# A Strassen mixer on one core: the second half's norm moved ahead of two early weight pairs, right factors made in the order of their products, four early pairs

## The chip, the cores and the metric

The kernel runs on one core of a Trainium2 chip. The core has a matrix engine (PE, with its weight loads PEld), a vector engine (DVE), an activation engine (ACT), a general engine (POOL) and a queue that issues DMAs (SP). Each engine takes its instructions strictly in the order of its own list, and waits for semaphores of the others. The metric is the time of one execution on the device in microseconds. Time before: 1500.17 us, the median of 3 runs (1498.93 to 1500.93).

## What is computed

A two-layer encoder trunk on 1024 tokens of width 1024, all in fp32. Layer 0 is attention and retention, layer 1 a gated short convolution; after each comes a cross-attention into 256 memory tokens. The change touches the entry of layer 1:

```
def conv_mixer(xn, w_in, conv_w, conv_b, w_out):
    gb, gc, u, gate = jnp.split(xn @ w_in, 4, axis=-1)      # w_in: 1024 x 4096
    z = gc * u
    conv = conv_b + (three taps over z along the tokens)
    y = gb * conv * jax.nn.silu(gate)
    return y @ w_out

x = x + conv_mixer(rmsnorm(x, o_norm), o_w_in, ...)          # x: sum of layer 0 and its cross-attention
```

## The kernel before

Activations lie transposed, 128 of the width on the partitions and the tokens along the free axis. An fp32 product is three passes on PE (`mm3`, L185 to L191): each operand is split in a high part, a cast by ACT, and a low part, a subtraction on DVE (`split`, L204 to L206), and hi*hi, hi*lo and lo*hi are summed. One such matmul is 128x128 by 128x512.

The product `xn @ w_in` is made in 16 **weight pairs** of two 128-column weight tiles each, and each pair as a 2x2 block product after Strassen and Winograd with 7 products instead of 8 (`strassen`, L611). The left factors come from the weights: A11, A12, A22 and the sums S1 to S4 (L99 to L102, on POOL), each cast by ACT and split by DVE (L106, L107) into a page; three `whi` and three `wlo` pages hold six factors in advance. The right factors come from the activations, the same ones for all 16 pairs: B11 and B21 from the first 512 tokens, and T1, T2, T3, B22, T4 from both halves (`right_factors`, L564; T1 = B12 - B11, T2 = B22 - T1, T3 = B22 - B12, T4 = B21 - T2). One product is 4 blocks of 3 matmuls, so 12 matmuls; a whole pair is 84.

The layer's input comes out of the previous output projection in two halves of 512 tokens (`out_proj_halves`, L301), each followed by its norm (`norm_half`, L265: add the last squares, split the sum, two matmuls by ones at L256 and L257, then Ln, Exp and Square on ACT and three steps on DVE, which give R) and by `right_factors` of that half, which first multiplies the tiles by gain and R (L575). With the first half done, only the products A11*B11 and A12*B21 of a pair can be made. Three pairs are begun with these two (`conv_start`, `EARLY` = 3): 24 matmuls each, from a weight tile that is loaded whole for this purpose. Everything that is left of these pairs ("late" products: T1, T2, T3, B22, T4 with their weight sums) and of the other 13 follows in `conv_in`.

Raw weight tiles go through two buffers (`wraw`), so the next pair's tiles are loaded once the present pair's sums and A22 are done with them. A product that adds to a sum in PSUM on which a copy (`kept`, by ACT, L623) has to be taken first waits for that copy.

The order on every engine is set by a scheduler at build time that simulates a timeline; the code's order is its starting point, and `issue_after` (used by the change) tells it what must be issued first. It decides where pieces of neighbouring pairs are interleaved.

Of the kernel before, what the change touches and what calls it, by code (L numbers as in the profile page):

```python
# [31 lines left out]
EARLY = 3  # L32
# [8 lines left out]
class Weights:  # L41
# [5 lines left out]
    FACTORS = ("A11", "A12", "S2", "S1", "S3", "S4", "A22")  # L47
# [88 lines left out]
class Trunk:  # L136
# [48 lines left out]
    def mm3(self, o, ah, al, bh, bl, first, last, more=False):  # L185
# [5 lines left out]
        mm(o, al, bh, start=False, stop=last, skip_group_check=more)  # L191
# [12 lines left out]
    def split(self, hi, lo, src, eng=None):  # L204
        self.nc.scalar.copy(hi, src)  # L205
        (eng or self.nc.vector).tensor_tensor(lo, src, hi.bitcast(F32), op=ALU.subtract)  # L206
# [15 lines left out]
    def rsqrt(self, var, out=None):  # L222
# [10 lines left out]
        nc.vector.tensor_tensor(out, t, r, op=ALU.mult)  # L233
# [17 lines left out]
    def mean(self, ones, sq):  # L251
# [5 lines left out]
        self.nc.tensor.matmul(ps, ones, w[:, 1, :n], start=False, stop=True)  # L257
# [306 lines left out]
    def right_factors(self, x, gain, h, out):  # L564
# [7 lines left out]
        for f in ("B11", "B21") if h == 0 else ("B12", "B22"):  # L572
# [5 lines left out]
        def split(f, src):  # L578
            for k in range(4):
# [8 lines left out]
                self.split(hi, lo, src[k])  # L588
                out.setdefault(f, []).append((hi, lo))

        if h == 0:
            split("B11", B["B11"])
            split("B21", B["B21"])
            return
# [15 lines left out]

    def strassen(self, B, out, early=False):  # L611
# [3 lines left out]
        def product(ps, f, first, weights=None):  # L615
            ah, al = weights or self.w.take()
            for k, (bh, bl) in enumerate(B[f]):
                c = slice(k * P, k * P + P)
                self.mm3(ps, ah[:, c], al[:, c], bh, bl, first and k == 0, k == 3, not first)
# [54 lines left out]
    def conv_start(self, B):  # L674

        self.started = []
        for i in range(EARLY):
            d = self.buf("v", "z" if i % 2 else "y1")
            self.started.append((d, self.times(B, d, None if i % 2 else AF.Silu, i)))
            next(self.started[-1][1])  # L680

    def conv_in(self, B):
# [3 lines left out]
        def pair(i):  # L686
# [5 lines left out]
            for _ in steps:  # L692
                pass
# [356 lines left out]
```

## Time and profile before

| | |
|---|---|
| median of 3 runs | 1500.17 us |
| the profiled execution | 1498.43 us |
| its span, first to last instruction | 1496.5 us |
| PE busy | 1442.0 us, 96% |
| DVE / ACT / POOL busy | 59% / 42% / 23% |
| PE busy from 820 to 860 us | 16.93 us of 40 |

The span is split by engine and in stretches of time; the granted clock of PE stands beside each stretch (1.00 is 2.4 GHz, 0.50 is 1.2 GHz). PE's matmuls are recorded with 0.39 us each, but at full speed the next one starts 0.227 us after the one before, so starts are what is to be counted.

### The profile page before, as it was taken

The page shows a single profiled execution, that of the slowest core. Times are in us where ns is not written, and L with a number is a line of the kernel's source. Part 1 is how long each engine was busy: PE and PEld are TensorE (multiplying, and loading weights), DVE is VectorE, ACT ScalarE, POOL GpSimd, SP SyncE. Part 2 cuts the span into 40 slices and gives each one's busy share as a digit, 9 for nine tenths or more (in the row PEclk, how much of TensorE's full clock was granted, in tenths as well). Part 3 has the DMA queues.
Part 4 walks back from the last instruction along what each step waited for, and adds up shares of the span by engine and source line. Part 5 has one row for each costly group of instructions (what it writes and reads, how often), then busy time and mean ns, then how long its engine had stood idle before and what let it go on. Part 6 is the DMA issues. An engine that isn't in the chain of part 4 may idle for free.

```text
span 1496.5 us, 18719 instructions
## 1 busy us (share of the span) xinstructions
PE 1442.0 (96%) x7218; PEld 1219.2 (81%) x7218; DVE 880.5 (59%) x1286; ACT 633.2 (42%) x1140; POOL 337.3 (23%) x205
## 2 busy tenths in 40 slices
PE   8999999999989999999999499999999999999996
PEld 6888888888788888888887288888888888888996
DVE  7656765566673356446465756666666336446555
ACT  6435662333363244345344333333344325335554
POOL 2300103233301210000114544444440120000233
PEclk9999999999999999999999599999999999999999
DMA  5411104211464521104754021111126532111464
GB/s 214 160 51 29 56 29 141 81 61 43 141 214 152 166 78 42 40 29 142 237 179 147 28 68 50 54 55 57 57 71 227 196 127 71 29 41 39 127 206 152
DMA packets 51482, 152.86 MB, mean 102 GB/s; under 512 B 6337, under 2 KB 14657, under 8 KB 50881
## 3 DMA queue, kind: packets, MB, share of 16 engines
q1 hardware_dynamic: 51392, 151.66, 31.8%
q8 instruction: 57, 0.93, 0.3%
q14 instruction: 33, 0.26, 0.1%
HBM read 122.28 MB, written 25.17 MB: 99 GB/s over the span
## 4 chain that ended last, share of the span: by engine, by line
PE 79%; DMA 6%; DVE 6%; POOL 3%; issue 3%; ACT 2%; SPq 0%; DVEq 0%; POOLq 0%; ACTq 0%
PE psd L189 16%; PE psd L191 16%; PE psd L190 16%; PE pssc L191 6%; PE pssc L190 6%; PE pssc L189 6%; PE psa L190 4%; PE psa L189 4%; PE psa L191 4%; DMA wraw<-w_o 1%; DMA swap<-bk 1%; PE pssc L367 1%; DMA swap<-bq 1%; PE psa L397 1%; PE psa L843 1%
## 5 line engine op out<-in xcount | busy, mean ns | idle before, releaser
L189 PE MATMUL psd<-xh,whi 128*128 128x512 f32 (+2 forms) x1096 | 414.1, 381 | 7.7 <-ACT whi L87 7.2
L190 PE MATMUL psd<-xl,whi 128*128 128x512 f32 (+2 forms) x1096 | 414.5, 379 | 0.0
L191 PE MATMUL psd<-xh,wlo 128*128 128x512 f32 (+2 forms) x1096 | 414.0, 379 | 0.0
L189 PEld LDWEIGHTS psd<-xh,whi 128*128 128x128 f32 x1096 | 206.5, 188 | 43.2 <-ACT whi L87 7.7
L191 PEld LDWEIGHTS psd<-xh,wlo 128*128 128x128 f32 x1096 | 206.2, 188 | 34.8
L190 PEld LDWEIGHTS psd<-xl,whi 128*128 128x128 f32 x1096 | 206.6, 189 | 34.0
L87 ACT CAST whi<-wraw 128x1024 fp32r<-128x1024 f32 (+1 forms) x134 | 139.8, 1044 | 212.3 <-PE psd L190 133.7
L249 POOL TENSOR_TENSOR ssq<-ssq,xold 128x512 f32<-128x512 f32 (+2 forms) x54 | 84.0, 1556 | 576.8 <-ACT xold L247 503.0
L88 DVE TENSOR_TENSOR wlo<-wraw,whi 128x1024 fp32r<-128x1024 f32 (+1 forms) x134 | 167.9, 1255 | 77.2 <-ACT whi L87 75.7
L106 ACT CAST wf<-ws 128x512 fp32r<-128x512 f32 x64 | 39.6, 622 | 138.5 <-PE pssc L191 81.5
L189 PE MATMUL pssc<-T,wf 128*128 128x512 f32 x180 | 71.7, 398 | 19.6 <-ACT T L205 9.9
L291 DVE TENSOR_TENSOR xnew<-psd,xold 128x512 f32<-128x512 f32 x32 | 21.9, 690 | 96.0 <-PE psd L191 92.6
L190 PE MATMUL pssc<-T,wf 128*128 128x512 f32 x180 | 71.8, 399 | 1.4 <-DVE T L206 1.4
L191 PE MATMUL pssc<-T,wf 128*128 128x512 f32 x180 | 71.0, 395 | 0.0
L247 ACT ACTIVATE xold<-xnew 128x512 f32<-128x512 f32 (+2 forms) x63 | 36.4, 580 | 70.2 <-DVE xnew L291 35.1
L107 DVE TENSOR_TENSOR wf<-ws,wf 128x512 fp32r<-128x512 f32 x64 | 49.6, 777 | 27.2 <-ACT wf L106 27.2
L107 DVE TENSOR_TENSOR wf<-wraw,wf 128x512 fp32r<-128x512 f32 x42 | 59.5, 1418 | 5.2 <-ACT wf L106 5.2
L189 PEld LDWEIGHTS pssc<-T,wf 128*128 128x128 f32 x180 | 34.4, 191 | 28.5 <-ACT T L205 10.3
L205 ACT CAST Th<-psa 128x512 fp32r<-128x512 f32 (+1 forms) x62 | 34.3, 588 | 54.5 <-PE psa L843 29.8
L99 POOL TENSOR_TENSOR ws<-wraw 128x512 f32<-128x512 f32 x16 | 38.9, 2429 | 69.2 <-DMA wraw<-w_o_in 61.9
L206 DVE TENSOR_TENSOR Tl<-psa,Th 128x512 fp32r<-128x512 f32 (+1 forms) x62 | 41.7, 687 | 21.4 <-ACT Th L205 21.1
L278 DVE TENSOR_TENSOR q<-psd,R 128x512 f32<-128x512 f32 x32 | 22.1, 690 | 53.9 <-PE psd L191 53.8
(319 smaller groups left out, 2975.4 us busy)
## 6 DMA issues: line engine op xcount, KB each, us to landing
wraw<-w_o SPq DMA_DIRECT2D x40, 512.0 KB, 3.9
wraw<-w_o_in SPq DMA_DIRECT2D x35, 512.0 KB, 3.6
wraw<-w_e_in SPq DMA_DIRECT2D x25, 512.0 KB, 3.9
wraw<-w_k SPq DMA_DIRECT2D x16, 512.0 KB, 4.1
xold<-x SPq DMA_DIRECT2D x16, 512.0 KB, 5.2
wraw<-w_v SPq DMA_DIRECT2D x16, 512.0 KB, 3.7
x<-xnew SPq DMA_DIRECT2D x16, 512.0 KB, 2.6
wraw<-w_q SPq DMA_DIRECT2D x16, 512.0 KB, 3.5
```

The lines of the kernel that those rows point to most:

```text
L87: self.nc.scalar.copy(hi[:, c], raw[:, c])
L88: self.nc.vector.tensor_tensor(lo[:, c], raw[:, c], hi[:, c].bitcast(F32), op=ALU.subtract)
L99: tt(F["S1"], F["A21"], F["A22"], op=ALU.add)
L106: self.nc.scalar.copy(hi, src)
L107: self.nc.vector.tensor_tensor(lo, src, hi.bitcast(F32), op=ALU.subtract)
L189: mm(o, ah, bh, start=first, stop=False, skip_group_check=more)
L190: mm(o, ah, bl, start=False, stop=False, skip_group_check=more)
L191: mm(o, al, bh, start=False, stop=last, skip_group_check=more)
L205: self.nc.scalar.copy(hi, src)
L206: (eng or self.nc.vector).tensor_tensor(lo, src, hi.bitcast(F32), op=ALU.subtract)
L247: nc.scalar.activation(sq, x, AF.Square)
L249: eng.tensor_tensor(self.ssq[:, a:b], self.ssq[:, a:b], sq, op=ALU.add)
```

## The change

`EARLY` goes from 3 to 4: a fourth pair is begun before the second half's right factors are there, with one more weight tile loaded whole. The early pairs 2 to 4 are to be issued behind the first early pair and behind the second half's norm (its ones-matmuls, its last activation and its last DVE step). `right_factors` of the second half makes each factor whole in turn: T1 (scale B12, subtract, split), T2 (scale B22, subtract, split), T3, B22, T4, each behind the one before. The products follow that order, T1's ahead of T2's in all pairs, and so the weight sum S1 comes ahead of S2. The sums of the first pair of `conv_in` are made by DVE instead of POOL. Unchanged lines are cut:

```diff
-EARLY = 3
+EARLY = 4
-    FACTORS = ("A11", "A12", "S2", "S1", "S3", "S4", "A22")
+    FACTORS = ("A11", "A12", "S1", "S2", "S3", "S4", "A22")
-            tt = self.nc.gpsimd.tensor_tensor
+            tt = (self.nc.vector if self.order[i][3:] else self.nc.gpsimd).tensor_tensor
...
-        for f in ("B11", "B21") if h == 0 else ("B12", "B22"):
+        def normed(f):
             for k in range(4):
...
-        for k in range(4):
-            tt(T1[k], B["B12"][k], B["B11"][k], op=sub)
-            tt(T2[k], B["B22"][k], T1[k], op=sub)
-        split("T2", T2)
-        split("T1", T1)
-        for k in range(4):
-            tt(T3[k], B["B22"][k], B["B12"][k], op=sub)
-        split("T3", T3)
-        split("B22", B["B22"])
-        for k in range(4):
-            tt(T4[k], B["B21"][k], T2[k], op=sub)
-        split("T4", T4)
+        def t1():
+            normed("B12")
+            for k in range(4):
+                tt(T1[k], B["B12"][k], B["B11"][k], op=sub)
+            return split("T1", T1)
+        def t2():
+            normed("B22")
+            for k in range(4):
+                tt(T2[k], B["B22"][k], T1[k], op=sub)
+            return split("T2", T2)
...
+        with ExitStack() as behind:
+            for make in (t1, t2, t3, lambda: split("B22", B["B22"]), t4):
+                last = make()
+                behind.enter_context(self.tc.issue_after(last.ins))
+                behind.enter_context(self.tc.issue_after(self.last_cast.ins))
...
-        product(a, "T2", False)
-        u2 = kept(a)
         c = self.ps("a")
         product(c, "T1", True)
         p5 = kept(c)
+        product(a, "T2", False)
+        u2 = kept(a)
         product(a, "T3", False)
...
+        with ExitStack() as behind:
+            for i in range(EARLY):
...
+                if i == 0:
+                    for x in (self.last_mean, self.last_act, self.last_rsqrt):
+                        behind.enter_context(self.tc.issue_after(x.ins))
+        self.last_early = self.last_mm
...
-                for i in range(0, len(o_in), 2)]
+                + ((True,) if i == 0 else ()) for i in range(0, len(o_in), 2)]
```

What this makes of the order shows at three places. In the rows a tile's last number is its own; `psa`, `psd` and `pssc` are PSUM tiles, `wf` a left factor, `ws` a tile of two sums, `xnew` the activations that are scaled in place.

**PE, around the norm's two ones-matmuls (L256, L257).** Before, they stand in the second early pair (`pssc_876`):

```order
L190 MATMUL pssc_876_6975<-B11_846_6611,whi83_6886 128x512
L256 MATMUL psa_868_6922<-sq2_867_6921,mean_dr_77 128x512
L191 MATMUL pssc_876_6975<-B11_846_6611,wlo83_6887 128x512
L189 MATMUL psd_877_6976<-B21_847_6614,whi83_6886 128x512
L190 MATMUL psd_877_6976<-B21_847_6614,whi83_6886 128x512
L257 MATMUL psa_868_6922<-sq2_867_6921,mean_dr_77 128x512
```

Now, right behind the last matmul of the first early pair (`psd_873`):

```order
L191 MATMUL psd_873_6937<-B21_850_6623,wlo82_6850 128x512
L256 MATMUL psa_868_6922<-sq2_867_6921,mean_dr_77 128x512
L257 MATMUL psa_868_6922<-sq2_867_6921,mean_dr_77 128x512
L189 MATMUL pssc_876_6973<-B11_843_6598,whi83_6886 128x512
L190 MATMUL pssc_876_6973<-B11_843_6598,whi83_6886 128x512
```

They stand 11 and 14 rows further ahead; three early pairs stand behind them now.

**DVE, from the scaling of the second half on, and POOL's sums.** Before, all eight tiles are scaled (L575), then the differences of all factors follow, and the first split (L206) comes 16 rows behind the last scaling:

```order
L575 SCALAR_TENSOR_TENSOR xnew_797_5992<-xnew_797_5992,gains_70,R_1_83 128x512
L575 SCALAR_TENSOR_TENSOR xnew_798_5993<-xnew_798_5993,gains_70,R_1_83 128x512
L599 TENSOR_TENSOR xnew_791_5986<-xnew_791_5986 128x512
L660 TENSOR_TENSOR y1_881_7016<-psd_883_7018,kept_884_7037 128x512
...
L608 TENSOR_TENSOR xnew_795_5990<-xnew_795_5990,T2_885_7061 128x512
L206 TENSOR_TENSOR T2_887_7071<-T2_885_7061,T2_887_7071 128x512
```

Now four tiles are scaled, and T1's first split comes eight rows later, with two of the sums of the first pair's weights (L99, L101) among them:

```order
L575 SCALAR_TENSOR_TENSOR xnew_794_5989<-xnew_794_5989,gains_70,R_1_83 128x512
L679 TENSOR_TENSOR z_875_6972<-psd_877_6974,kept_878_6995 128x512
L604 TENSOR_TENSOR xnew_791_5986<-xnew_791_5986 128x512
L604 TENSOR_TENSOR xnew_792_5987<-xnew_792_5987 128x512
L604 TENSOR_TENSOR xnew_793_5988<-xnew_793_5988 128x512
L99 TENSOR_TENSOR ws_882_7013<-wraw86_1_6981 128x512
L101 TENSOR_TENSOR ws_882_7013<-wraw86_0_6979,wraw86_1_6981 128x512
L604 TENSOR_TENSOR xnew_794_5989<-xnew_794_5989 128x512
L206 TENSOR_TENSOR T1_891_7099<-xnew_791_5986,T1_891_7099 128x512
```

On POOL the four sums of the first pair are gone, and the second pair's (`ws_908`, `ws_909`, from `wraw87`) stand first.

**PE, where the second pair's late products begin, and ACT's copy ahead of T3.** Before, two matmuls of the second pair (`pssc_876`, left factor `wf90`) stand in the middle of the first pair's T1 (`psa_906`):

```order
L189 MATMUL psa_906_7165<-T1_890_7086,wf86_6986 128x512
L189 MATMUL pssc_876_6975<-T2_887_7071,wf90_7148 128x512
L190 MATMUL pssc_876_6975<-T2_887_7071,wf90_7148 128x512
L190 MATMUL psa_906_7165<-T1_890_7086,wf86_6986 128x512
L191 MATMUL psa_906_7165<-T1_890_7086,wf86_6986 128x512
```

Now two of the second pair's T1 (`psa_913`, left factor `wf91`, its S1) stand between the first pair's B22 and its T4:

```order
L191 MATMUL psa_907_7171<-B22_902_7152,wf89_7059 128x512
L189 MATMUL psa_913_7274<-T1_891_7099,wf91_7185 128x512
L190 MATMUL psa_913_7274<-T1_891_7099,wf91_7185 128x512
L189 MATMUL pssc_872_6936<-T4_903_7159,wf90_7172 128x512
L190 MATMUL pssc_872_6936<-T4_903_7159,wf90_7172 128x512
```

On ACT the copy for which the first pair's T3 waits stands behind all casts of T3 and B22 now:

```order
L205 CAST T3_898_7140<-xnew_794_5989 128x512
L205 CAST B22_899_7143<-xnew_795_5990 128x512
L205 CAST B22_900_7146<-xnew_796_5991 128x512
L205 CAST B22_901_7149<-xnew_797_5992 128x512
L205 CAST B22_902_7152<-xnew_798_5993 128x512
L642 COPY kept_911_7217<-pssc_872_6936 128x512
L205 CAST T4_903_7159<-xnew_795_5990 128x512
```

So 17 late matmuls of the first pair stood ahead of the second pair's first two before, and 48 stand there now. In the last eleven pairs (the sixth to the sixteenth) the order is now: nine matmuls of T1, T4 of the pair before (12), three of T1, T2 (12), two of the next pair's first product, B22 (12, with S4), eight of the next pair's first product, T3 (12). Before, B22 and its S4 came 49 matmuls behind the T4 of the pair before.

## Rows read from the trace of the kernel before

**Rows 1.** Two stretches: busy PE, PEld, DVE, ACT, POOL, then PE's clock, DMA, GB/s.

```profile
820.00:860.00 40.00, 16.93 (x42) 10.54 (x41) 32.22 (x52) 16.60 (x30) 21.50 (x4) 0.62 0.09 26
860.00:1496.50 636.50, 624.20 (x3048) 534.72 (x3046) 367.82 (x447) 256.67 (x431) 173.03 (x111) 0.99 0.30 96
```

**Rows 2.** PE's waits, whole span: for whom, us in total, times, longest.

```profile
PE pssc L189 <- ACT T L205: 9.9, 1, 9.9
PE pssc L189 <- ACT wf L106: 9.0, 1, 9.0
```

**Rows 3.** PE in order of time: start, us, operation, and idle time before it.

```profile
804.45 0.39 PE L189 MATMUL pssc<-B,whi 128*128 128x512 f32 x1
...
818.05 0.39 PE L190 MATMUL psd<-B,whi 128*128 128x512 f32 x1
...
821.40 0.39 PE L191 MATMUL psd<-B,wlo 128*128 128x512 f32 x1
...
841.50 0.63 PE L190 MATMUL psa<-T,wf 128*128 128x512 f32 x1
...
843.63 0.63 PE L189 MATMUL psa<-T,wf 128*128 128x512 f32 x1
...
853.28 0.80 PE L189 MATMUL pssc<-T,wf 128*128 128x512 f32 x1 [9.03 <-ACT wf L106]
...
858.16 0.50 PE L189 MATMUL pssc<-T,wf 128*128 128x512 f32 x1 [0.68 <-ACT kept L623]
```

**Rows 4.** Single microseconds; behind the five engines' times stands PE's granted clock.

```profile
824.00:825.00 1.00, 0.00 (x0) 0.00 (x0) 1.00 (x3) 0.00 (x0) 0.00 (x0) 0.54 0.00 0
...
858.00:859.00 1.00, 0.83 (x4) 0.70 (x5) 0.35 (x2) 1.00 (x3) 0.00 (x0) 0.90 0.00 0
```

**Rows 5.** DVE in order of time, from the last early weight tile on.

```profile
805.55 1.23 DVE L88 TENSOR_TENSOR wlo<-wraw,whi 128x1024 fp32r<-128x1024 f32 x1 [0.21 <-ACT whi L87]
...
808.07 0.69 DVE L206 TENSOR_TENSOR sq<-ssq,sq 128x512 fp32r<-128x512 f32 x1 [0.69 <-ACT sq L205]
...
817.42 0.69 DVE L231 SCALAR_TENSOR_TENSOR rt<-psa,rt 128x512 f32<-128x512 f32 x1 [0.68 <-ACT rt L230]
...
821.37 5.39 DVE L575 SCALAR_TENSOR_TENSOR xnew<-xnew,gains,R 128x512 f32<-128x512 f32 x8
826.67 0.69 DVE L599 TENSOR_TENSOR xnew<-xnew 128x512 f32<-128x512 f32 x1
...
841.11 2.49 DVE L206 TENSOR_TENSOR T<-xnew,T 128x512 fp32r<-128x512 f32 x4
...
847.13 1.89 DVE L206 TENSOR_TENSOR T<-xnew,T 128x512 fp32r<-128x512 f32 x3
```

**Rows 6.** ACT in order of time, at the norm and at the splits.

```profile
814.85 0.62 ACT L106 CAST wf<-ws 128x512 fp32r<-128x512 f32 x1 [2.33 <-POOL ws L100]
815.38 0.69 ACT L228 ACTIVATE rs<-psa,eps 128x512 f32<-128x512 f32 x1
...
837.57 2.17 ACT L205 CAST B<-xnew 128x512 fp32r<-128x512 f32 x4
...
857.53 0.58 ACT L623 COPY kept<-pssc 128x512 f32<-128x512 f32 x1 [0.24 <-PE pssc L191]
```

**Rows 7.** POOL in order of time: the sums of the first and the second pair.

```profile
810.58 1.29 POOL L99 TENSOR_TENSOR ws<-wraw 128x512 f32<-128x512 f32 x1 [8.04 <-DMA wraw<-w_o_in]
...
832.35 17.79 POOL L99 TENSOR_TENSOR ws<-wraw 128x512 f32<-128x512 f32 x1 [16.16 <-DMA wraw<-w_o_in]
850.10 1.26 POOL L101 TENSOR_TENSOR ws<-wraw,wraw 128x512 f32<-128x512 f32 x1
```

**Rows 8.** Raw weight tiles, 780 to 900 us: times from a DMA's issue to its landing.

```profile
DMA to landing us min/median/max: 3.4/3.6/7.2
```

**Rows 9.** Sum tiles: cast and low part of a left factor, ns min/median/max over 64 of each.

```profile
L106 ACT CAST wf<-ws x64: 617/622/631, 811.9 to 1127.4; 128x512 fp32r<-128x512 f32 x64
L107 DVE TENSOR_TENSOR wf<-ws,wf x64: 673/692/1384, 812.6 to 1128.1; 128x512 fp32r<-128x512 f32 x64
```

More of the change, by code (lines that the diff above doesn't have):

```diff
@@ L190, in mm3 @@
         mm(o, ah, bl, start=False, stop=False, skip_group_check=more)
-        mm(o, al, bh, start=False, stop=last, skip_group_check=more)
+        self.last_mm = mm(o, al, bh, start=False, stop=last, skip_group_check=more)
     def dense(self, xs, done, parts=((0, H), (H, S)), tags="d"):
@@ L204, in split @@
     def split(self, hi, lo, src, eng=None):
-        self.nc.scalar.copy(hi, src)
-        (eng or self.nc.vector).tensor_tensor(lo, src, hi.bitcast(F32), op=ALU.subtract)
+        self.last_cast = self.nc.scalar.copy(hi, src)
+        return (eng or self.nc.vector).tensor_tensor(lo, src, hi.bitcast(F32), op=ALU.subtract)
     def split_k(self, src, gain=None, two=False):
@@ L232, in rsqrt @@
         nc.vector.tensor_scalar(t, t, -0.5, 1.5, ALU.mult, ALU.add)
-        nc.vector.tensor_tensor(out, t, r, op=ALU.mult)
+        self.last_rsqrt = nc.vector.tensor_tensor(out, t, r, op=ALU.mult)
         return out
@@ L256, in mean @@
         self.nc.tensor.matmul(ps, ones, w[:, 0, :n], start=True, stop=False)
-        self.nc.tensor.matmul(ps, ones, w[:, 1, :n], start=False, stop=True)
+        self.last_mean = self.nc.tensor.matmul(ps, ones, w[:, 1, :n], start=False, stop=True)
         return ps
@@ L587, in split @@
                     hi, lo = t[:, :H], t[:, H:]
-                self.split(hi, lo, src[k])
+                last = self.split(hi, lo, src[k])
                 out.setdefault(f, []).append((hi, lo))
+            return last
         if h == 0:
-            split("B11", B["B11"])
-            split("B21", B["B21"])
+            for f in ("B11", "B21"):
+                normed(f)
+                split(f, B[f])
             return
@@ L597, in right_factors, with t3, t4 @@
         T2 = [t[:, i, :] for t in (self.buf("T", "T2", (P, 2, H)) for _ in range(2)) for i in range(2)]
-        for k in range(4):
-            tt(T1[k], B["B12"][k], B["B11"][k], op=sub)
-            tt(T2[k], B["B22"][k], T1[k], op=sub)
-        split("T2", T2)
-        split("T1", T1)
-        for k in range(4):
-            tt(T3[k], B["B22"][k], B["B12"][k], op=sub)
-        split("T3", T3)
-        split("B22", B["B22"])
-        for k in range(4):
-            tt(T4[k], B["B21"][k], T2[k], op=sub)
-        split("T4", T4)
+        def t1():
[8 more added lines that the diff above has]
+            return split("T2", T2)
+        def t3():
+            for k in range(4):
+                tt(T3[k], B["B22"][k], B["B12"][k], op=sub)
+            return split("T3", T3)
+        def t4():
+            for k in range(4):
+                tt(T4[k], B["B21"][k], T2[k], op=sub)
+            return split("T4", T4)
+        with ExitStack() as behind:
[3 more added lines that the diff above has]
+                behind.enter_context(self.tc.issue_after(self.last_cast.ins))
     def strassen(self, B, out, early=False):
@@ L616, in product @@
             ah, al = weights or self.w.take()
-            for k, (bh, bl) in enumerate(B[f]):
-                c = slice(k * P, k * P + P)
-                self.mm3(ps, ah[:, c], al[:, c], bh, bl, first and k == 0, k == 3, not first)
+            with self.tc.issue_after(self.last_mm.ins) if early == 0 and early is not False else ExitStack():
+                for k, (bh, bl) in enumerate(B[f]):
+                    c = slice(k * P, k * P + P)
+                    self.mm3(ps, ah[:, c], al[:, c], bh, bl, first and k == 0, k == 3, not first)
         def kept(ps):
@@ L676, in conv_start @@
         self.started = []
[L677 to L680, printed above, removed]
+        with ExitStack() as behind:
+            for i in range(EARLY):
+                d = self.buf("v", "z" if i % 2 else "y1")
+                self.started.append((d, self.times(B, d, None if i % 2 else AF.Silu, i)))
+                next(self.started[-1][1])
+                if i == 0:
+                    for x in (self.last_mean, self.last_act, self.last_rsqrt):
+                        behind.enter_context(self.tc.issue_after(x.ins))
+        self.last_early = self.last_mm
     def conv_in(self, B):
@@ L691, in pair @@
                 steps = self.times(B, d, None if i % 2 else AF.Silu)
-            for _ in steps:
-                pass
+            if i == 0:
+                self.last_mm = self.last_early
+            with self.tc.issue_after(self.last_early.ins) if i < EARLY else ExitStack():
+                for _ in steps:
+                    pass
             return d
```

## The prediction

> **What bounds the kernel now.** I read the stretches first. PE is busy 624.20 of the 636.5 us behind 860, but 16.93 of the 40 us from 820 to 860, with a mean clock of 0.62 [rows 1]. The list of PE's waits then names the causes: one of 9.9 us for a cast of a right factor, one of 9.0 for the cast of a left factor [rows 2]. PE's own timeline gives the price. 60 matmuls lie between 804.45 and 818.05, so one takes 0.2267 us at full clock, and the last of the three early pairs starts at 821.40 [rows 3]. In the program's order 26 late matmuls stand ahead of the one that starts at 858.16; from there PE runs at its own pace. So the stretch 821.63 to 858.16 holds 26 x 0.2267 = 5.9 us of work and **30.6 us of loss**. The clock has part in it: it fell to 1.2 GHz at about 824.5, and was back at 2.4 GHz at about 858.1, 4.8 us after PE's resumption at 853.28 [rows 3, 4]; in between a matmul took (843.63 - 841.50) / 5 = 0.426 us [rows 3].
>
> What PE waits for is read from the other engines. DVE works without a gap from the norm's last steps (817.42) to 849.02 [rows 5]. The first wait ends when T2's first cast comes, behind all eight scalings and T1's four differences. The second ends with the second pair's S2: POOL's first sum started at 832.35 and took 17.79 us where the first pair's took 1.29 [rows 7]. It ended at 850.14, 1.1 us behind DVE's last instruction. So two things set the loss: how early DVE's train begins and in which order it makes the factors, and where it ends.
>
> **The change, step by step.** The sum is made on the trace's time axis, up to the point from which PE runs freely.
>
> *The norm moves ahead.* The first early pair ends at 804.45 + 24 x 0.2267 = 809.9. The low part of the sum of squares is ready at 808.76 [rows 5], so the two ones-matmuls behind that pair wait for nothing; the second ends at 810.5. Ln started at 815.38 before, since ACT stood at a cast that waited for a POOL sum until 814.85 [rows 6]; both casts of weight sums ahead of it are gone, so it starts at 810.6. DVE's first step came 2.04 us behind Ln [rows 5, 6], now at 812.65: the train begins 4.8 us sooner. Three steps more and the first pair's sum follow at up to 0.60 each, and R is there at 814.8.
>
> *The fourth early pair* gives PE 24 matmuls of cover, until 821.63 + 24 x 0.2267 = 827.1; they are taken from later, so they cost nothing. Its weight tile needs one cast and one low part (1.23 us [rows 5]), which stands on DVE ahead of the scalings: these start at 816.0. It replaces four half-size steps later on engines that PE does not wait for. Its raw tile holds one of the two raw buffers until that step, so the first pair's second tile is issued at 816.05 and lands 3.6 us later, the median [rows 8]: 819.7.
>
> *DVE's train.* From 816.0 to the last split of T4 there stand 8 scalings of 0.66 us (821.37 to 826.67 for eight) and 49 other steps of 0.60 (four in 2.49, three in 1.89) [rows 5]: the 36 differences and splits of the second half, 4 sums of weights that were POOL's, 5 low parts of left factors, and 4 additions for results. That is 5.3 + 29.6 = 34.9 us, so it ends at 850.9. The four sums cost 2.4 us here. Left on POOL they would meet the train, since the tile lands at 819.7, and the row of 17.79 us [rows 7] shows what that means. The first sum stands where DVE arrives at 821.1, 1.4 us behind the landing; landings took up to 7.2 us [rows 8], which would stop the train for 2.2 us.
>
> *PE along the train.* T1's four splits are whole at 827.7 and the last is needed at 829.4, so T1 runs from 827.1 to 829.8 without a wait. T2's first low part comes 4 scalings and 10 other steps later, at 836.4: PE idles 6.6 us and the clock falls, as it did in the gap from 821.8. T2's eleven further matmuls at 0.426 us end at 841.1. T3 must wait for ACT's copy of T2's sum, which stands behind the casts of T3 and B22: the last T3 difference ends at 840.6, its cast at 841.2, four B22 casts take 2.17, the copy 0.58 [rows 6]: 843.9. T3 and B22 are 24 matmuls; with the first 4.8 us at 1.2 GHz (11 matmuls) and the rest at 2.4 GHz they end at 851.7.
>
> *The second pair's S1.* Two matmuls of the second pair stand ahead of the first pair's T4, and they need POOL's first sum. Its tiles go out when DVE is through with A22, at about 832.9, and land at 836.5, inside the train. I take the nearest row: the sum ends 1.1 us behind DVE's last step [rows 5, 7], at 852.1. With a cast of 0.62 [rows 9] and the hand-overs PE goes on at 852.8. The 14 matmuls up to the end of T4 take 3.2 us: 856.0.
>
> Of the Trainium skill, the page "SBUF — State Buffer", section "SBUF: two separate sides", has a rule that bears on this: DVE and POOL share one port pair as an exclusive lock that goes to whichever instruction starts first, for that whole instruction. The rows agree that one blocks the other, but not that POOL gets a turn between two DVE instructions, since some 27 of them passed a waiting sum. By the rule in its plain form the sum would be done soon after 837 and the time would be that of the first rival.
>
> *The sum.* By 856.0 PE has done 62 late matmuls behind the early ones, 62 x 0.2267 = 14.1 us of work from 827.1 on: **14.9 us of loss in place of 30.6**, so 15.7 us gained.
>
> *What comes after.* The third pair's S1 is next in line: POOL's other sums (1.26 us for the second [rows 7]) and A22's split end at about 856.9, a tile lands at 860.5, the sum and its cast end at 862.5, and PE arrives 34 matmuls behind 856.0, at 863.7. It has 1.2 us to spare; a landing of 7.2 us would cost 2.4. The reordered products in later pairs move no work on or off PE, and T1's and T2's copies lie 14 and more matmuls ahead of their use. Between the ends of this I take zero, and keep the 2.4 for the range.
>
> **From profile to median.** The profiled execution took 1498.43 us, 1.9 more than its span; the median of the runs is 1500.17. The gain is taken from the median: 1500.17 - 15.7 = **1484.5 us**.
>
> **Rivals.** *POOL gets a turn early, and the clock stays up.* If the second pair's first sum slips in between DVE's steps, PE goes on at 851.7 instead of 852.8; 1483.4. If the clock also stays at 2.4 GHz, B22 ends at 843.9 + 5.4 = 849.3, and T4 is held by its last split at 850.9: it ends at 851.4, 4.6 us sooner than forecast, 1479.9. Against it speaks that nothing of the sort happened in the train before.
>
> *The clock stays low and a tile lands late.* With all of T3, B22, the two and T4 at 0.426 us (38 matmuls, 16.2 us) T4 ends at 860.1, 4.1 us later: 1488.6; with the late landing at the first sum 1490.8. In favour: PE's gaps of 6.6 and 2.8 us. Against: the row of 858, where 4.8 us of work sufficed.
>
> *The train is longer than its rows.* If some of its steps run beside ACT and wait for a cast each, or the DMA of the second pair comes after the train, the weights of pairs two and three arrive late as well; 5 to 8 us are lost, 1489 to 1493. DVE waited for no cast in the train before.
>
> *Slower: each later pair waits for S4.* In the last eleven pairs B22 now comes 17 matmuls behind the T4 whose page S4 takes over: 3.9 us to the first use, 4.3 to that of the low part, where it was 49 matmuls. A cast (0.62) and a low part (0.69, at most 1.38) [rows 9] need 1.4 to 2.1 us. PE loses only what exceeds 4.3; the gain is gone when S4 takes 4.3 + 15.7 / 11 = 5.7 us, and at 6.5 us the kernel takes 1508. It would need a queue ahead of these two steps; in the order both stand right behind A22's, ahead of the long steps of the convolution.
>
> **How the numbers follow.** About 0.2%, 3 us, is what a measurement here can tell from no change. The forecast with the clock and landing as in the rows 0.60; the early turn of POOL 0.13; the low clock or the late landing 0.12; the longer train 0.06; S4's wait enough to undo the gain 0.09, of which 0.05 slower and 0.04 within 0.2%. The forecast's own bounds and the first two rivals give 1479.5 to 1491, which leaves out about 0.15 to 0.2. Faster 0.91, same 0.04, slower 0.05.
>
> **What would show it.** In the profile after: ones-matmuls at about 810, Ln at about 810.6, scalings at 816; T1 on PE at about 827 with no wait; a wait of some 6 us for T2's split, one of 2 to 3 for the copy ahead of T3, and a short one for the left factor of the second pair; POOL's first sum again over 10 us long and ending about 1 us behind DVE's train; full pace from about 856. It is wrong if DVE stands at its first weight sum (late tile), if T4 waits long for a left factor, or if waits of PE at B22 with a `wf` cast repeat every 19 us.

## The result: 1484.3 us in place of 1500.5

The changed kernel took 1484.28 us, the median of 4 runs (1482.23 to 1486.66); the kernel before took 1500.49 us beside it (4 runs, 1498.93 to 1500.93). The ratio is 0.9894, with a 95% interval of 0.9877 to 0.9912. The forecast was 1484.5 us within 1479.5 to 1491. A second set of runs on another occasion gave 1484.05 against 1498.51, ratio 0.9904 (0.9887 to 0.9920). The profiled execution of the changed kernel took 1482.23 us with a span of 1480.1.

First the two stretches that answer [rows 1] (busy PE, PEld, DVE, ACT, POOL, then PE's clock, DMA, GB/s):

```profile
820.00:860.00 40.00, 31.02 (x113) 22.97 (x111) 34.88 (x53) 18.38 (x32) 21.88 (x7) 0.87 0.17 52
860.00:1480.10 620.10, 605.54 (x2960) 518.15 (x2960) 357.33 (x439) 252.24 (x424) 163.03 (x109) 0.99 0.30 97
```

PE was busy 16.93 of these 40 us before and is busy 31.02 now; its clock went from 0.62 to 0.87. The work behind 860 is the same in kind. The list of PE's waits from 820 to 900 answers [rows 2]:

```profile
PE pssc L189 <- ACT T L205: 4.2, 1, 4.2
PE pssc L189 <- ACT kept L642: 2.4, 1, 2.4
PE pssc L190 <- DVE T L206: 1.9, 1, 1.9
PE psd L189 <- DVE second L686: 1.0, 1, 1.0
PE psa L189 <- ACT wf L106: 0.7, 2, 0.5
PE psa L191 <- DVE wf L107: 0.4, 1, 0.4
```

The 9.9 us for T2's cast have become 4.2 + 1.9, the 9.0 us for the left factor 0.27 at the second pair (of the 0.7 in the fifth line), and the copy ahead of T3 costs 2.4. Three waits further back are new: two at the third pair, one for an addition.

PE in order of time, as in [rows 3]: the first early matmul, T1's first and last, T2's first two, T3's first, the second pair's first late one, the end of T4, the waits behind it, and the 480th matmul of the stage.

```profile
801.33 0.39 PE L189 MATMUL pssc<-B,whi 128*128 128x512 f32 x1
...
823.93 0.39 PE L189 MATMUL psa<-T,wf 128*128 128x512 f32 x1
...
826.42 0.39 PE L191 MATMUL psa<-T,wf 128*128 128x512 f32 x1
831.00 0.50 PE L189 MATMUL pssc<-T,wf 128*128 128x512 f32 x1 [4.18 <-ACT T L205]
833.36 0.79 PE L190 MATMUL pssc<-T,wf 128*128 128x512 f32 x1 [1.86 <-DVE T L206]
...
840.78 0.50 PE L189 MATMUL pssc<-T,wf 128*128 128x512 f32 x1 [2.38 <-ACT kept L642]
...
848.40 0.50 PE L189 MATMUL psa<-T,wf 128*128 128x512 f32 x1 [0.27 <-ACT wf L106]
...
851.50 0.39 PE L191 MATMUL pssc<-T,wf 128*128 128x512 f32 x1
...
860.26 0.50 PE L189 MATMUL psa<-T,wf 128*128 128x512 f32 x1 [0.46 <-ACT wf L106]
...
861.39 0.50 PE L191 MATMUL psa<-T,wf 128*128 128x512 f32 x1 [0.41 <-DVE wf L107]
...
883.99 0.50 PE L189 MATMUL psd<-T,wf 128*128 128x512 f32 x1 [1.01 <-DVE second L686]
...
926.97 0.39 PE L190 MATMUL psa<-B,wf 128*128 128x512 f32 x1
```

The whole stage begins 3.12 us sooner in this execution (801.33 against 804.45). To compare executions I therefore measure from the first early matmul and call **loss** what the stage took beyond its work: the time to the 480th matmul less 479 x 0.22667 us. Here it is 926.97 - 801.33 - 108.57 = **17.07 us**; before it was 944.33 - 804.45 - 108.57 = **31.31**, with the 480th matmul here:

```profile
944.33 0.39 PE L189 MATMUL pssc<-B,wf 128*128 128x512 f32 x1
```

So the stage itself gave 14.2 us.

DVE and POOL at the end of the train, which answers [rows 5, 7]:

```profile
844.66 1.88 DVE L206 TENSOR_TENSOR T<-xnew,T 128x512 fp32r<-128x512 f32 x3
846.47 0.68 DVE L686 TENSOR_TENSOR second<-pssc,kept 128x512 f32<-128x512 f32 x1
847.07 1.18 DVE L206 TENSOR_TENSOR T<-xnew,T 128x512 fp32r<-128x512 f32 x1
```

```profile
834.20 13.49 POOL L99 TENSOR_TENSOR ws<-wraw 128x512 f32<-128x512 f32 x1 [34.67 <-DMA wraw<-w_o_in]
847.66 1.73 POOL L101 TENSOR_TENSOR ws<-wraw,wraw 128x512 f32<-128x512 f32 x1
```

POOL's first sum of the second pair was held up again, but it ended at 847.69, inside DVE's row and not 1.1 us behind it.

### The profile page after: what moved, and what is told of

Its sections match the earlier page's. It is cut to its first block, busy times and chain, and to the rows that moved or that the text cites. A ratio compares the mean times of both kernels' runs of the same rounds, so it can differ in the third digit from the quotient of the medians.

```text
span 1480.1 us, 18711 instructions
## 1 busy us (share of the span) xinstructions
PE 1438.2 (97%) x7218; PEld 1215.4 (82%) x7218; DVE 878.1 (59%) x1289; ACT 634.8 (43%) x1139; POOL 322.7 (22%) x201
## 4 chain that ended last, share of the span: by engine, by line
PE 79%; DVE 8%; DMA 5%; POOL 3%; issue 2%; ACT 2%; SPq 0%; DVEq 0%; POOLq 0%; ACTq 0%
PE psd L191 17%; PE psd L189 17%; PE psd L190 17%; PE pssc L191 5%; PE pssc L189 5%; PE pssc L190 5%; PE psa L190 4%; PE psa L189 4%; PE psa L191 4%; DMA swap<-bk 1%; PE pssc L367 1%; DMA swap<-bq 1%; PE psa L397 1%; PE psa L871 1%; POOL bk L432 1%
## 5 line engine op out<-in xcount | busy, mean ns | idle before, releaser
L189 PE MATMUL pssc<-T,wf 128*128 128x512 f32 x168 | 67.1, 399 | 6.6 <-ACT T L205 4.2
L190 PE MATMUL pssc<-T,wf 128*128 128x512 f32 x168 | 67.2, 400 | 1.9 <-DVE T L206 1.9
L191 PE MATMUL pssc<-T,wf 128*128 128x512 f32 x168 | 66.9, 398 | 0.0
L107 DVE TENSOR_TENSOR wf<-wraw,wf 128x512 fp32r<-128x512 f32 x40 | 55.1, 1393 | 5.0 <-ACT wf L106 5.0
L206 DVE TENSOR_TENSOR Tl<-psa,Th 128x512 fp32r<-128x512 f32 (+1 forms) x62 | 41.7, 686 | 21.4 <-ACT Th L205 21.1
L99 POOL TENSOR_TENSOR ws<-wraw 128x512 f32<-128x512 f32 x15 | 32.0, 2131 | 90.5 <-DMA wraw<-w_o_in 90.5
L189 PE MATMUL psd<-y,whi 128*128 128x512 f32 x128 | 50.0, 391 | 0.0
```

The costliest lines, as they stand in the source:

```text
L189: mm(o, ah, bh, start=first, stop=False, skip_group_check=more)
L190: mm(o, ah, bl, start=False, stop=False, skip_group_check=more)
L191: self.last_mm = mm(o, al, bh, start=False, stop=last, skip_group_check=more)
L206: return (eng or self.nc.vector).tensor_tensor(lo, src, hi.bitcast(F32), op=ALU.subtract)
```

## The experiments

Every experiment is the changed kernel with one edit (the last two in the table with a second edit on top of it), and none leaves a computation out. All measured losses stand in one table; the first and the last matmul are those between which the loss is measured. Each ratio is to the kernel before in the same set of runs, whose median was 1500.49, 1498.04, 1498.51 or 1500.54 us; so it is the ratios and the losses that compare across the rows, not the medians.

| kernel | first, 480th matmul | loss, us | median, us | ratio to before (95%) |
|---|---|---|---|---|
| before | 804.45, 944.33 | 31.31 | 1500.49 | 1 |
| changed | 801.33, 926.97 | 17.07 | 1484.28 | 0.9894 (0.9877-0.9912) |
| changed, again | 804.93, 930.73 | 17.23 | 1484.05 | 0.9904 (0.9887-0.9920) |
| norm not held ahead | 803.66, 931.33 | 19.10 | 1485.19 | 0.9915 (0.9901-0.9930) |
| three early pairs | 804.35, 933.17 | 20.25 | 1488.94 | 0.9933 (0.9919-0.9947) |
| first sums on POOL | 805.13, 933.22 | 19.52 | 1487.40 | 0.9925 (0.9912-0.9939) |
| old order of factors | 802.93, 928.72 | 17.22 | 1484.82 | 0.9906 (0.9892-0.9921) |
| T2's copy on DVE | 802.47, 927.04 | 16.00 | 1481.99 | 0.9892 (0.9876-0.9909) |
| T1's copy on DVE | 805.34, 931.08 | 17.17 | 1485.09 | 0.9912 (0.9897-0.9927) |
| second sums on DVE | 806.15, 929.17 | 14.45 | 1481.67 | 0.9883 (0.9863-0.9903) |
| that, and T2's copy on DVE | 802.84, 926.33 | 14.92 | 1481.79 | 0.9883 (0.9866-0.9900) |
| second sums on DVE, S3, S4, A22 late | 802.68, 924.49 | 13.24 | 1480.69 | 0.9870 (0.9854-0.9887) |

The loss repeats to 0.2 us in two executions of the changed kernel, while the runs of one kernel spread by 1.3 to 5.3 us. The theory that the runs test (the last experiments show that it holds as a floor only): **the row of DVE's steps sets the end of the stage; POOL's sums come through only where that row lets them; PE's order and its clock fill what is left.**

### The changed kernel once more

> The changed kernel once more, for the spread of one profiled execution. Theory (the 3.1 us by which the profiled execution of the changed kernel was ahead when the first early pair began is chance, since nothing is changed there): the first early matmul anywhere from 801 to 805.5 us, while the loss behind it is within 0.5 of 17.1. Rival (the change also quickens what lies ahead of the early pairs): the first early matmul at 801 to 802.

The first early matmul came at 804.93, 3.6 us later than in the first profile, and the loss was 17.23. So the 3.1 us by which the first profile was ahead are chance: over the eleven profiles of kernels with the same early part it lay anywhere from 801.33 to 806.15.

### Each part of the change taken back

*The norm not held ahead of the later early pairs:*

```
-                if i == 0:
-                    for x in (self.last_mean, self.last_act, self.last_rsqrt):
-                        behind.enter_context(self.tc.issue_after(x.ins))
```

> The changed kernel, but without the three lines that hold the later early pairs behind the second half's norm; the planner then puts the two ones-matmuls behind the second early pair's matmuls (11 and 13 of them) and nine short steps of DVE (weight sums, low parts, two additions) ahead of the scalings. Theory (DVE's train decides, the norm's start only as far as DVE would stand idle): DVE's first norm step comes 3.2 us later than 809.48, T1 waits 1 to 2 us on PE, but T2's first low part comes within 0.5 us of where it was (832.6), since the 3.8 us for which DVE waited there are filled with steps that it has to do anyway. Time within 1.5 us of the changed kernel's 1484.3. Rival (each microsecond by which the norm starts later is a microsecond of the train): T2's first low part 3 us later, time about 1487.5.

The loss rose by 2.0 us, between the two, and the median of 1485.19 us lay within the theory's 1.5 us. DVE shows why (in this kernel 803.66 is the first early matmul):

```profile
815.00 0.69 DVE L99 TENSOR_TENSOR ws<-wraw 128x512 f32<-128x512 f32 x1 [3.57 <-DMA wraw<-w_o_in]
...
816.81 0.68 DVE L231 SCALAR_TENSOR_TENSOR rt<-psa,rt 128x512 f32<-128x512 f32 x1
```

Three sums (L99, L101, L100) now stand ahead of the norm's first step L231, and DVE stood 3.6 us at the first of them for its tile. L231 came 13.15 us behind the first early matmul where it was 8.15 (809.48 - 801.33): 5.0 us later, not 3.2. T2's first low part came 1.9 us later. So 3.1 of 5.0 us were absorbed by steps that DVE had done meanwhile; the first theory's mechanism holds in part, its size did not: the start came 1.8 us later than it said, for the tile, and T2's low part 1.9.

*Three early pairs* (`EARLY = 3`):

> The changed kernel with three early pairs instead of four. Theory (cover is worth its work on PE, less what it costs DVE): PE ends the early pairs 5.4 us sooner and waits about 4 us for T1; DVE's train loses the fourth tile's low part and one addition, 1.8 us, so the first pair's T4 ends some 1.8 us sooner, but 24 matmuls (5.4 us) are still to be done: 3.6 us longer, 1487.9, with 1487 to 1489.5 as bounds. Rival (the train alone decides, and later waits swallow what PE has in hand): no loss, 1482.5 to 1484.5.

The loss rose by 3.2 us, the time to 1488.94, as the theory said. The fourth early pair is 5.4 us of PE work in the gap, less what its tile costs DVE. PE waited 1.0 and 3.8 us for T1.

*The first pair's sums on POOL again:*

```
-                + ((True,) if i == 0 else ()) for i in range(0, len(o_in), 2)]
+                for i in range(0, len(o_in), 2)]
```

> The changed kernel with the first pair's four weight sums on POOL, as in the kernel before. Theory (while DVE runs instructions with two inputs in SBUF one after the other, POOL's addition waits; it gets in when DVE runs one with an input in PSUM, or stands still): POOL's first sum starts at about 817 and ends at about 820 to 821, behind the addition of an early result; DVE stands at the low parts of S1 and S3 for some 2 us each, POOL's other sums run in these gaps, and 2.4 us of DVE work are saved: 1.5 to 4 us longer than the changed kernel, 1486 to 1488. Rival one (POOL gets a turn between any two DVE instructions): sums of 1.3 to 2 us each, all through by 825, no stop of DVE: about 1 us shorter, 1483. Rival two (the price is that of the row of 17.8 us for each sum that meets the train): more than 10 us longer.

The loss rose by 2.5 us, 1487.4: the theory's case, and neither of the two rivals. POOL, then DVE beside it:

```profile
820.51 3.67 POOL L99 TENSOR_TENSOR ws<-wraw 128x512 f32<-128x512 f32 x1 [17.34 <-DMA wraw<-w_o_in]
```

```profile
822.94 0.68 DVE L679 TENSOR_TENSOR y<-psd,kept 128x512 f32<-128x512 f32 x1
824.87 1.11 DVE L107 TENSOR_TENSOR wf<-ws,wf 128x512 fp32r<-128x512 f32 x1 [1.24 <-ACT wf L106]
```

The sum waited from 820.51, ended 1.24 us behind the start of the addition L679, and DVE stood 1.24 us at the low part of S1 (not at that of S3, as the theory also had it; two of T1's low parts took 1.78 us instead). The prediction had pointed to the row of 17.79 us for this case; here the sum took 3.67 us, because an addition with a PSUM operand stood near and because DVE soon waited itself.

*The old order of right factors and products* (T2's product first, the planner free to mix the steps of all factors):

```
-            for make in (t1, t2, t3, lambda: split("B22", B["B22"]), t4):
-                last = make()
-                behind.enter_context(self.tc.issue_after(last.ins))
-                behind.enter_context(self.tc.issue_after(self.last_cast.ins))
+        normed("B12")
+        normed("B22")
+        for k in range(4):
+            tt(T1[k], B["B12"][k], B["B11"][k], op=sub)
+            tt(T2[k], B["B22"][k], T1[k], op=sub)
+        split("T2", T2)
+        split("T1", T1)
...
```

> The changed kernel with the right factors made and multiplied in the order of the kernel before (T2's product first, the planner free to mix the factors' steps, weight sums in the old order); norm, four early pairs and sums on DVE stay. Theory (DVE's train and the kept copies set the end, and PE's order only fills the gap): T2's first low part at about 834.6, PE waits some 10.5 us for it, then T2 and T1 run on; the copy of T2's sum stands behind casts of T4's factors, so T3 starts at about 843, but at the full clock: T4 ends within 2 us of 851.7, time 1483 to 1486.5. Rival (doing T1 within the gap is the point of the new order): T1's 2.7 us come on top, and the longer gap keeps the clock low through T3: 1488 to 1491.

The loss was 17.22, the changed kernel's own. PE waited 1.6 and 7.5 us for T2's split, the second of these until 1.2 us later than the theory had it (837.36, or 835.8 on the changed kernel's times, against 834.6). But then T2 and T1 ran on, T3 came at the full clock, and the later waits were short. With the other three parts in place, the order of the factors, which is most of the diff, is worth nothing.

The four parts, each taken back alone, cost 2.0 + 3.2 + 2.5 + 0.2 = 7.9 us of the 14.2. The rest would show only if several were taken back together, which no run did; how it divides stays open.

### When does POOL get through?

*The copy of T2's sum on DVE:*

```
-            self.nc.scalar.copy(t, ps)
+            (self.nc.vector.tensor_copy if dve else self.nc.scalar.copy)(t, ps)
...
-        u2 = kept(a)
+        u2 = kept(a, early == 0 and early is not False)
```

> The changed kernel, but the copy of T2's sum of the first pair (ahead of T3 on PE) is made by DVE instead of ACT; the planner puts it between the third and the fourth low part of T3. It reads PSUM and writes SBUF, so it has no input in SBUF. Loss here is the time from the first early matmul less 0.2267 us for each matmul since, read at the 480th: 31.3 before, 17.1 in the changed kernel. Theory (POOL's addition gets in where DVE runs an instruction with at most one input in SBUF): POOL's first sum of the second pair starts at about 33 us behind the first early matmul, as before, but ends at 39 to 40.5 instead of 46.4, behind this copy; T3 starts about 0.7 us sooner; the second pair's left factors are early, and the third pair's waits of 1.2 us go: loss 14 to 16, time 1481 to 1483.5. Rival one (POOL gets in only at the end of the row of DVE's instructions, or at the addition of T3's result, whatever else DVE runs): the sum ends at 46 to 48 as in the changed kernel, loss 16 to 17. Rival two (DVE now stands at the addition of B22's result, which the planner puts ahead of T4's last low parts): T4 ends later, loss 17 to 18.5.

DVE and POOL of this kernel:

```profile
838.57 1.89 DVE L206 TENSOR_TENSOR T<-xnew,T 128x512 fp32r<-128x512 f32 x3
840.38 0.68 DVE L642 COPY kept<-pssc 128x512 f32<-128x512 f32 x1
840.98 1.16 DVE L206 TENSOR_TENSOR T<-xnew,T 128x512 fp32r<-128x512 f32 x1
```

```profile
835.17 6.42 POOL L99 TENSOR_TENSOR ws<-wraw 128x512 f32<-128x512 f32 x1 [34.66 <-DVE T L206]
841.55 1.73 POOL L101 TENSOR_TENSOR ws<-wraw,wraw 128x512 f32<-128x512 f32 x1
847.00 1.58 POOL L100 TENSOR_TENSOR ws<-ws,wraw 128x512 f32<-128x512 f32 x1 [3.73 <-ACT T L205]
```

The sum ended at 841.59, 39.1 us behind the first early matmul and 1.21 us behind the start of the copy, 7.2 us sooner than in the changed kernel: the theory's number, and rival one falls. T3 started 0.7 us sooner and the third pair's waits went. The loss fell by 1.1 us only, to the edge of what was expected, since POOL's sums, now in the middle of DVE's row, held up four of its steps by 0.5 to 1.1 us each, and PE waited 1.39 us for T4's cast.

*The copy of T1's sum on DVE*, the control, 3 us ahead of POOL's request (the same edit at `p5 = kept(c)`):

> The changed kernel, but the copy of T1's sum of the first pair is made by DVE instead of ACT; the planner puts it behind the second of T2's four differences, some 29.5 us behind the first early matmul and 3 us ahead of the moment at which POOL's first sum of the second pair can start. Theory: POOL has nothing to run at that moment, so the sum is as late as in the changed kernel, it ends at 46.5 to 47.5; the copy only lengthens DVE's row by 0.6 us: loss 17.3 to 18, time 1484.3 to 1485.5. Rival (any copy taken from ACT to DVE gives POOL room, or ACT's casts were what the products waited for): the sum ends before 42, or loss below 16.8.

POOL's sum ended at 47.0 us behind the first early matmul, again 1.23 us behind the start of L686, and T2's low part came 0.6 us later, both as the theory said. The loss (17.17) stayed 0.1 below its range: it was 0.6 us higher up to T4 and 1.4 behind the third pair's waits, but PE then came that much later to the place of the wait at 883.99 and did not wait there.

*The second pair's sums on DVE too* (`if i == 0` becomes `if i <= 2` in the line that puts the first pair's there; the index counts tiles):

> The changed kernel with the second pair's four weight sums on DVE too, as the change does it for the first pair. The planner puts two of them behind T4's differences and two among T4's low parts. Theory (POOL's late sum is no longer waited for in the changed kernel: 0.27 us at the second pair's first left factor; what is worth something is that the second pair's raw tiles are free sooner): T4's last low part comes 1.3 us later without holding PE up, the second pair's low parts run at 0.6 us each, the third pair's waits of 1.2 us go: loss 15.4 to 16.5, time 1482.5 to 1483.5. Rival (four steps more in DVE's row are 2.4 us more ahead of T4): loss 18 to 19.5.

The loss fell to 14.45, 1.0 below what the theory gave: no wait of PE is left behind T3's start. Up to T4's last matmul it was 14.4 against 14.1 in the changed kernel, so the whole gain lies behind T4.

```profile
PE pssc L189 <- ACT T L205: 4.2, 1, 4.2
PE pssc L189 <- ACT kept L642: 2.4, 1, 2.4
PE pssc L190 <- DVE T L206: 1.6, 1, 1.6
```

This is the list of PE's waits in this kernel from 820 to 940. On DVE a sum costs 0.6 us. On POOL the four sums cost DVE 2.8 us in held-up steps in the changed kernel (from 847.07 on four steps took 1.18, 1.56, 1.56 and 1.18 us in place of 0.68), and everything behind them came late.

### Is the loss the waits, or the row of DVE's steps?

*The last three left factors of the first pair behind the right factors that come first* (on top of the second pair's sums on DVE; the core of the edit):

```
             for make in (t1, t2, t3, lambda: split("B22", B["B22"]), t4):
...
+                if make in (t2, t3):
+                    self.w.hold = None
+                    self.w.prepare(self.w.next + (make is t3))
```

> The kernel with the second pair's sums on DVE, and in addition the first pair's last three left factors put behind the right factors that come before them: S3 behind T2's low parts, S4 and A22 behind T3's. Five steps of DVE (3.0 us) move from ahead of T2's first low part to behind it; the sum of its steps stays. Loss is again the time from the first early matmul less 0.2267 us for each matmul, at the 480th (31.3 before, 17.1 changed kernel, 14.5 with the second pair's sums on DVE). Theory (the end of DVE's row sets the end of T4, whatever PE waits for on the way): T2 starts about 3 us sooner, at 28.5 behind the first early matmul, PE's gap ahead of it shrinks to about 3.5 us and the clock falls later or not at all, T3 starts at about 35 instead of 39.5; but T4's last low part stays at 48 to 49, PE waits for S4 and for T4's low parts instead: loss 13.3 to 14.5, time 1480.5 to 1482. Rival (the waits and the slow clock are the loss): 3 us of waits and 2 to 4 us of clock are gained: loss 9 to 11.5, time 1476 to 1479.

PE's waits from 820 to 940 (this kernel's lines lie lower: L200 to L202 are the matmuls, L216 and L217 the split, L114 the low part of a left factor, L658 the copy):

```profile
PE psa L202 <- DVE wf L114: 2.5, 1, 2.5
PE pssc L200 <- ACT T L216: 2.2, 1, 2.2
PE pssc L201 <- DVE T L217: 1.8, 4, 1.3
PE psa L200 <- ACT wf L113: 1.1, 2, 0.9
PE pssc L200 <- ACT kept L658: 1.0, 1, 1.0
```

and PE's granted clock, the third number from the right, around T2:

```profile
833.00:834.00 1.00, 1.00 (x4) 0.81 (x3) 1.00 (x3) 0.00 (x0) 0.00 (x0) 0.50 0.00 0
...
835.00:836.00 1.00, 1.00 (x3) 0.35 (x2) 1.00 (x3) 1.00 (x3) 0.00 (x0) 0.59 0.00 0
836.00:837.00 1.00, 0.07 (x1) 0.00 (x0) 1.00 (x3) 1.00 (x3) 0.00 (x0) 1.00 0.00 0
```

T2's second matmul came 29.0 us behind the first early one in place of 32.0, T3 at 34.4 in place of 39.5, and T3 ran at the full clock. Yet the loss fell by 1.2 us only, to 13.24, 0.06 below the theory's range and far from the rival's 9 to 11.5. PE gave the rest back at B22, where it waits 2.5 us for S4's low part, and at T4, whose last low part ended at 851.50, 48.8 us behind the first early matmul; with the second pair's sums alone it was 48.2. PE waited for T4's third and fourth low part (0.16 and 0.24 of the 1.8 us in the third line), so here the end of DVE's row does set the end of T4.

In the two kernels with which it is compared it does not. T4's last low part lay ready at 848.25 in the changed kernel, 3.0 us ahead of PE's matmul on it at 851.28, and 2.0 us ahead with the second pair's sums on DVE. There PE's own chain set the end: the wait for T2's low part, the slow clock, the copy ahead of T3. So the rival had a part of the loss right, but the end of the row lies close below it as a floor, and taking waits away won 1.2 us before the floor was reached.

At 1480.69 us (0.9870) this is the lowest time of the study, though its interval overlaps that of the second pair's sums alone.

*Both: the second pair's sums and T2's copy on DVE:*

> The second pair's sums on DVE and the copy of T2's sum on DVE together. Theory (as for the run with late S3): the copy is one more step in DVE's row, 0.6 us; T3 starts 0.7 us sooner, but T4's last low part comes as late or later: loss 13.9 to 14.8, no gain over the second pair's sums alone. Rival (the copy is worth what it was worth by itself, 1.1 us of loss, on top): loss 13.2 to 13.6.

The loss was 14.92, 0.5 more than without the copy and 0.1 beyond the theory's range: T3 started 0.7 us sooner again, and that bought nothing.

## Why the forecast held, step by step

All times of the prediction are on the axis of the profile before; 3.12 us are to be taken off for the profile after.

**The norm.** Ln was forecast for 810.6 and came at 807.42 + 3.12 = 810.5; DVE's first step L231 for 812.65, and it came at 809.48 + 3.12 = 812.60; the scalings for 816.0, at 812.88 + 3.12 = 816.0. The tile for the first pair's sums had landed before DVE came to them.

**T1, T2, T3.** T1 for 827.1 without a wait: 827.05, none. T2's first low part for 836.4: PE's matmul on it began at 836.48. T3 behind the kept copy for 843.9: 843.90. These hang on counting DVE's rows and on ACT's order, and both were right to 0.1 us. The row itself was to end at 850.9 and ended at 848.25 + 3.12 = 851.37; the difference is what POOL's sum held up its last step (1.18 us in place of 0.68).

**The clock** fell to half rate in T2's gap, was back just behind T2, fell again as T3 began and was back at 845, so that T2's last eleven matmuls and some nine of T3 ran at 1.2 GHz. The single microseconds (columns as in [rows 4], PE alone):

```profile
831.00:832.00 1.00, 0.50 (x1) 0.72 0.80 119
838.00:839.00 1.00, 0.41 (x1) 0.87 0.00 0
841.00:842.00 1.00, 1.00 (x5) 0.84 0.00 0
845.00:846.00 1.00, 1.00 (x6) 0.95 0.00 0
```

The prediction had T2's eleven and 11 matmuls of T3 at half rate; that the clock would rise and fall once more between them it did not say, and against the forecast it cost nothing: B22 ended at 847.98 + 3.12 = 851.10 in place of 851.7. In reading the trace of before it was loose at one place, which enters no term: by the 0.54 of the microsecond from 824 to 825 [rows 4] the clock fell at about 824.1 and not 824.5, and it was up from about 844.4 to 848, while PE stood.

**The second pair's S1: the step that was mis-sized.** The prediction let POOL's sum end 1.1 us behind DVE's last step, at 852.1; it ended at 847.69 + 3.12 = 850.8, 1.3 us sooner. It got through at L686, the only step of that stretch with an operand in PSUM. PE, there 0.6 us sooner than forecast, waited 0.27 us for the left factor and went on at 848.40 + 3.12 = 851.52 in place of 852.8. The rivals had "POOL gets a turn early" with 0.13 and 851.7 for this point, so that part of the rival came true; the prediction had argued against it from a row in which DVE ran no step with an operand in PSUM. T4 ended at 851.73 + 3.12 = 854.85 in place of 856.0. The loss at that point, by the prediction's own sum, was 854.85 - 827.05 - 62 x 0.2267 = 13.7 and not 14.9.

**What comes after: the term taken as zero.** It cost 2.9 us (14.1 us of loss at T4's last matmul, 17.07 at the 480th). The third pair's S1 was said to have 1.2 us to spare. PE came 1.2 us sooner, which took the margin; the tile came later too (POOL's sum began at 858.27 + 3.12 = 861.39 in place of 860.5), so that the cast ended at 863.32 and not 862.5, and the low part took 1.10 us in place of 0.69. Some 1.4 us went there. Another 1.2 went at 883.99 to an addition L686 that stood on DVE behind two steps of the convolution, and 0.2 just behind T4. The run with the second pair's sums on DVE shows all of them gone, and the run with T2's copy on DVE, where POOL's sum was 7.2 us sooner, all but 0.4 us; that POOL's late sums are their cause is shown, by which of the steps between is not.

So the stage gave 31.3 - 17.1 = 14.2 us where 15.7 was forecast: +1.2 at T4, -2.9 behind it, and 0.2 of rounding in the two ways of counting. The medians differ by 16.2 us in one set of runs and 14.5 in the other, which is the same within their spread. That the forecast of the median lay 0.2 us off is luck to that extent.

**The rivals.** The later pairs' S4: no wait for a left factor of 0.2 us or more behind 930, and from the 480th matmul to the end of the span it took 553.1 us against 552.2 before and 552.6 in the second profile, so no more than 0.9 us was lost there, and the other kernels differ by more (551.4 to 553.2). By its own terms S4 at 6.5 us would have given 1508.7 us and not 1508. The longer train and the late tile did not occur in the changed kernel; the late tile did in the run without the held norm, with 3.6 us. The clock stayed low no longer than forecast.

## What to carry to other kernels

Where several engines feed one gap, find the engine whose row of steps has no idle time from its first input to the gap's end, and count that row: its end is a floor for the gap's end. What is lost above the floor hangs on where single steps stand in the row: T2's first low part came 1.9 us later with the norm not held and the loss rose by 2.0, while two weight sums more ahead of T4's low parts and one among them ended the row 1.3 us later and cost 0.3 at T4. An early start is worth what the row's engine would otherwise stand idle, and no more if a load lies in between. A margin of about a microsecond behind a stage that is to become faster is not a margin: price the next wait with the new arrival time, not with the old one.

## What was new of the hardware

An addition of two SBUF inputs that POOL began while DVE ran steps with two inputs in SBUF, one each 0.60 us, mostly waited: for 12 us and more in the kernel before, the changed one and four others. It ended 1.1 to 1.2 us behind the moment at which DVE began a step with an operand in PSUM, or stopped. The starts of such steps and the ends of the sums: 846.47 and 847.69 (changed), 840.38 and 841.59 (T2's copy), 822.94 and 824.18 (sums on POOL), 851.07 and 852.30 (T1's copy), 850.73 and 851.95 (norm not held), and 854.43 and 855.67 for another of POOL's additions (in the kernel with S3, S4 and A22 late, where its line is L699; it took 5.23 us). With three early pairs it was the end of the row, 848.43, and the sum ended at 849.59:

```profile
845.94 2.49 DVE L206 TENSOR_TENSOR T<-xnew,T 128x512 fp32r<-128x512 f32 x4
850.28 1.12 DVE L107 TENSOR_TENSOR wf<-ws,wf 128x512 fp32r<-128x512 f32 x1 [1.84 <-ACT wf L106]
```

```profile
831.71 17.88 POOL L99 TENSOR_TENSOR ws<-wraw 128x512 f32<-128x512 f32 x1 [29.32 <-DVE wf L107]
```

The Trainium skill, page "SBUF — State Buffer", section "Who interferes with whom", says that a DVE instruction with at most one SBUF input does not contend with GpSimd outside its two-port modes, and that one with two does if the GpSimd instruction reads SBUF; these ends agree.

Other rows speak against a plain rule. With T2's copy on DVE, POOL's sum L100 began at 847.00 and took 1.58 us, while DVE was in four differences with two SBUF inputs each:

```profile
845.55 3.58 DVE L620 TENSOR_TENSOR xnew<-xnew,T 128x512 f32<-128x512 f32 x4
```

Four such steps take 2.49 us elsewhere, and taken one by one it is the last of them that took 1.78 us: POOL came in between the third and the fourth. In the same kernel its addition L683, begun at 852.76, came in behind one such step as well. And where one addition of POOL follows directly on another, POOL and DVE take turns. In the changed kernel, with no step on DVE from 884.99 to 890.10 that has an operand in PSUM:

```profile
886.70 3.48 DVE L107 TENSOR_TENSOR wf<-wraw,wf 128x512 fp32r<-128x512 f32 x2
```

```profile
886.18 1.74 POOL L99 TENSOR_TENSOR ws<-wraw 128x512 f32<-128x512 f32 x1
887.88 1.74 POOL L101 TENSOR_TENSOR ws<-wraw,wraw 128x512 f32<-128x512 f32 x1
```

So the long wait was that of an addition that came new into a running row. What let in the two of the kernel with T2's copy, and not those that waited, stays open; it was not tried.
